# A first group of six columns, fewer GpSimd splits, two load queues, products of zeros and later latent norms in a two-layer decoder trunk

## The chip, the cores and the metric

The kernel runs on one core of one Trainium2 chip. The metric is the device time of one execution in microseconds (us), the median of several runs. The core has five engines with a row of instructions each: TensorE (PE: matrix products and transpositions; PEld is its weight load), VectorE (DVE), ScalarE (ACT), GpSimd (POOL) and SyncE (SP), which here issues loads and stores. An engine works through its own row in order; an instruction waits until what it needs from other engines is there, and all behind it wait too.

## The reference

A trunk of two layers over 512 tokens of width 1024, in fp32. Each layer normalises x, projects it by one wide matrix, feeds four causal token mixers, gates and sums their outputs, and ends with a SwiGLU block. Cut to what the change touches:

```python
for l in range(DEPTH):                      # DEPTH = 2
    h = rmsnorm(x, norm1_g[l])
    p = split_columns(h @ w_in[l])          # a_q ... c_q, c_kv, c_kr, d_q ... d_iq, d_ik, gate
    ...
    # C: q = rmsnorm(c_q) @ w_uq ; kv = rmsnorm(c_kv) @ w_ukv      (latents of 384 and 256 columns)
    # D: ik = apply_rope(rmsnorm(d_ik)) ; the index scores pick the keys
    # B: values b_vs, b_vw and gates b_g of the native sparse attention
    ...
    x = x + jnp.sum(g * br, axis=2) @ w_out[l]
    h2 = rmsnorm(x, norm2_g[l])
    gate, up = jnp.split(h2 @ w_gate_up[l], 2, axis=-1)
    x = x + (jax.nn.silu(gate) * up) @ w_down[l]
return rmsnorm(x, final_norm_g)
```

## The kernel before

x lies transposed, as eight tiles of 128 rows (model dimension) by 512 tokens. Every operand of a matrix product is split into a high and a low part (`fp32r`), and a product of two blocks is three instructions: high by high, high by low, low by high (`mm3`). "Product" below means one such instruction. A column of 128 outputs over eight tiles of x is so 24 products of 128x512.

**Weights.** They stream in as loads of 128x1024 (`raw`, three buffers), eight blocks each, in the order in which the code asks for blocks. `weights` (line 326) splits a half load, four blocks, at a time: ScalarE writes the high part `wp`, and VectorE subtracts for the low part; each third half is GpSimd's instead (`POOL_EVERY`). Six `wp` buffers take turns, and the splits run up to three halves ahead.

**The order.** Python code plays the program through once and writes the rows of all engines. A main path issues the products; beside it run tasks (generators) which `tick` advances when a planned time is due: a string that a task yields ("v", "a", "g", "p") means to come back when that engine's planned work is done, a number means so many us of planned time. These planned times set the order alone; on the chip only the order and the waits are left.

**PSUM.** Three banks `mm`, two `sc`, two `tr`, one `pv`. A bank given back in the code is reused by the next holder, which waits until the last reader is through.

**Start of a layer** (`mixers`, line 1264). `gather(GROUP)` makes the first GROUP columns one group: for each tile k of x the products of all these columns follow each other (`dense_group`, line 386). The first columns are the keys (c_kr with d_ik), three of c_q and two of c_kv. With a group of four, the two of c_kv follow one by one, 24 products each. Then come the token products (`native_values` by `values` and `dense_tokens`, line 414): x is the stationary side, 276 columns wide, one bank for each 128 tokens, in the order `mm`, `mm`, `pv`, `sc`; 12 products for each of eight tiles. Then the index queries `d_iq` (four columns) and gates.

**Norms.** h is fed unnormalised, and the scale is applied to the results. `rstd` (line 569) makes it: four small products with ones (a statistic, tile `tr<-ones,sq`), then on VectorE twelve small steps of 128x4 (`rx`, `ri`, `ry`, `ra`; here the "root"), then four transpositions `tr<-ident,ry`, from which ScalarE copies `R`. This is done for x, for the keys (`keys`, line 842), and for the latents c_q and c_kv (`latent`, line 1210, by `norm_row`, line 589). `plain` (line 833) multiplies a finished bank by R into `pl` and gives the bank back.

**Names in the rows.** `h` the split x, `sq` squares and their sums, `pl` a normalised column, `sh`, `rk`, `ro` the rope, `sk` and `kl` the high and low parts of the index keys, `lat` the normalised latents, `v`, `G`, `IW` the values and gates read from the token products' banks, `tab` rope tables, `z0` the zeros, `x0` the first x.

**Start of the program** (`run`, line 1512). GpSimd fills masks and constants (`setup`); SP issues, in this order, the first half load, `aux` (gains), the first tile of x, the second half load, and the other tiles of x with two loads between.

Of the kernel before, what the change touches and what calls it, by code (L numbers as in the profile page):

```python
# [11 lines left out]
F32 = mybir.dt.float32  # L12
F32R = mybir.dt.float32r
# [5 lines left out]
P = 128  # L19
S = 512  # L20
NQ = S // P
# [129 lines left out]

PL, LAT, BG, BGS = 1.0, 0.3, 5, 0.5
XR, TD, LD = 1.2, 6, 0.5
LOOK, ZC, NFT, GROUP = 3, 4, 16, 4
NKEEP = (NF - NFT) * KT // 4
N_U, N_RAW, N_WP, POOL_EVERY = 67, 3, 6, 3
BANKS = {"mm": 3, "sc": 2, "tr": 2, "pv": 1}


# [38 lines left out]
class Body:  # L198
# [127 lines left out]
    def weights(self, half):  # L326

        nc = self.nc
        total = 2 * NUNITS
        while self.nhalf <= min(half + min(LOOK, 1 + max(half, 0)), total - 1):  # L330
            h = self.nhalf
            while self.nraw <= min(h // 2 + N_RAW - 1, NUNITS - 1):
                self.load_raw()
            r = self.raws[h // 2][:, (h % 2) * S:(h % 2) * S + S]
            if h < total - NKEEP:
                w = self.sbt([P, 2, S], "wp", N_WP, "wp", F32R)
                w = w[:, 0, :], w[:, 1, :]
            else:
                w = self.pair("wk")
            self.wps[h] = w  # L340
            nc.scalar.activation(w[0], r, AF.Copy)
            pool = h % POOL_EVERY == POOL_EVERY - 1
            (nc.gpsimd if pool else nc.vector).tensor_tensor(w[1], r, w[0].bitcast(F32), op=ALU.subtract)
            if h % 2:
                del self.raws[h // 2]
            self.nhalf += 1
# [38 lines left out]

    def dense_group(self, group, pairs, k0=0, c=slice(0, S)):

        ps = [self.main_bank(tag) for tag in ("mm", "mm", "mm", "sc")[:len(group)]]
        last = len(pairs) - 1
        for k, x in enumerate(pairs):  # L390
            x = self.get(x)
            for i, (spec, cols, post, t) in enumerate(group):
                m = len(cols)
                w = self.block(spec[:2] + (k0 + k,), cols, spec[2:])
                self.mm3(ps[i][:m, c], w, (x[0][:, c], x[1][:, c]), k == 0, k == last)
                if k == last:
                    self.task(post(ps[i]), PL, t)
                self.tick()
# [167 lines left out]
            v.scalar_tensor_tensor(y, a, 1.5, y, op0=ALU.add, op1=ALU.mult)  # L566
        return y

    def rstd(self, sq, dim, rows=slice(0, P), blocks=range(NQ)):

        tr, ident = self.nc.tensor, self.ident
        ps = yield from self.bank("tr")
        yield from self.turn()
        for b in blocks:
            tr.matmul(ps[:, b:b + 1], sq[rows, b * P:(b + 1) * P], self.ones[rows, :], start=True, stop=True)
        yield 0.3
        n, b0 = len(blocks), blocks[0]
        col = self.rsqrt(ps[:, b0:b0 + n], n, dim)
        self.rel(ps)
        yield "v"  # L580
        yield 1.5
        ps = yield from self.bank("tr")
        yield from self.turn()
        for b in blocks:
            tr.transpose(ps[:, b * P:(b + 1) * P], col[:, b - b0:b - b0 + 1].to_broadcast([P, P]), ident)
        yield "p"
        return ps, col

    def norm_row(self, st, dim, n):
        yield from self.until(lambda: st.get("n") == n)  # L590
        yield "v"
        ps, col = yield from self.rstd(st["s"], dim)
        r = self.u("R")
        self.nc.scalar.activation(r, ps, AF.Copy)
        self.rel(ps)
        return r, col
# [32 lines left out]
        return out  # L629

    def load_tab(self, i):
        c, s = (self.sbt([P, S], "tab", 4, "tab") for _ in range(2))
        self.nc.sync.dma_start(c, self.tabs[i])
        self.nc.sync.dma_start(s, self.tabs[i + 1])
        return c, s
# [12 lines left out]
    def setup(self):  # L648
        nc, sb = self.nc, self.sb
        self.ident = sb.tile([P, P], F32, name="ident")  # L650
        nc.gpsimd.memset(self.ident, 1.0)
        nc.gpsimd.affine_select(out=self.ident, in_=self.ident, pattern=[[-1, P]], base=0, channel_multiplier=1,
                                compare_op=ALU.is_equal, fill=0.0)

        self.kls = [[sb.tile([P, S], F32R, name=f"kl{i}{h}") for h in range(2)] for i in range(2)]
        for kl in self.kls:
            for h in range(2):
                nc.gpsimd.memset(kl[h][64 - 64 * h:128 - 64 * h].bitcast(F32), 0.0)
        self.ones = sb.tile([P, 1], F32, name="ones")
        nc.vector.memset(self.ones, 1.0)  # L660

        self.TM = sb.tile([P, S], F32, name="TM")
        nc.gpsimd.memset(self.TM, 0.0)
        nc.gpsimd.affine_select(out=self.TM[:, S - P:], in_=self.TM[:, S - P:], pattern=[[-1, P]], base=0,
                                channel_multiplier=1, compare_op=ALU.is_ge, fill=BIG)

        self.CM = sb.tile([P, NQ, 32], F32, name="CM")
        nc.gpsimd.memset(self.CM, 0.0)
        for b in range(NQ):
            nc.gpsimd.affine_select(out=self.CM[:, b, :], in_=self.CM[:, b, :], pattern=[[-16, 32]],  # L670
                                    base=b * P - 31, channel_multiplier=1, compare_op=ALU.is_ge, fill=BIG)
        nc.gpsimd.memset(self.CM[:, :, 31:32], BIG)
        self.ZM = sb.tile([P, NQ], F32, name="ZM")
        nc.gpsimd.memset(self.ZM, 1.0)
        nc.gpsimd.affine_select(out=self.ZM, in_=self.ZM, pattern=[[P, NQ]], base=-31, channel_multiplier=1,
                                compare_op=ALU.is_ge, fill=0.0)

    def load_aux(self, l, eng=None):
        a = self.sb.tile([P, NAUX], F32, name=f"aux{l}", tag="aux", bufs=1)
# [162 lines left out]
    def keys(self, l, t1):  # L842

        nc = self.nc
        t1 = yield from self.aw(t1)
        tx = self.load_tab(TAB_X)
        hi, lo = slice(64, P), slice(0, 64)
        sq = self.u("sq")
        nc.scalar.activation(sq[hi], t1[hi], AF.Square)
        yield "a"  # L850
        ps, _ = yield from self.rstd(sq, 64, hi)
        rm = self.sbt([P, S], "xr", 3, "rm")
        nc.gpsimd.memset(rm[lo], 1.0)
        nc.scalar.activation(rm[hi], ps[hi], AF.Copy)
        self.rel(ps)
        yield "a"
        nc.vector.scalar_tensor_tensor(t1, t1, self.ax(l, "gm"), rm, op0=ALU.mult, op1=ALU.mult)
        r = yield from self.rope(t1, tx, self.u("rk"), False)
        ks = [self.stack_hi(r, h) for h in range(2)]
        yield "a"  # L860
        out = []
        for h, s in enumerate((lo, hi)):
            kl = self.u("kl", F32R)
            for o in (lo, hi):
                nc.gpsimd.tensor_tensor(kl[o], r[s], ks[h][s].bitcast(F32), op=ALU.subtract)
            out.append((ks[h], kl))
        yield "g"
        return out
# [341 lines left out]
    def latent(self, l, ts, dim, gname):  # L1210

        st, xs = {}, []
        for t in ts:
            x = yield from self.aw(t)
            xs.append(x)
            sq = self.norm_sq(x)
            yield "a"
            self.norm_add(st, sq)
        r, _ = yield from self.norm_row(st, dim, len(ts))
        yield "a"  # L1220
        out = []
        for i, x in enumerate(xs):
            self.nc.gpsimd.tensor_tensor(x, x, r, op=ALU.mult)
            yield "g"
            out.append(self.task(self.split(x, self.ax(l, gname, i), "lat"), 0))
        return out
# [185 lines left out]
    def out_proj(self, l, src, ap):  # L1412
        nc = self.nc
        st = {}
        xs, hs = [], []
        self.gather(3)
        for m in range(KT):
# [5 lines left out]
                yield "v"  # L1423
                return (yield from self.feed(l, "g2", m, x, st))
            xr = self.xr
            xr[m] = self.sbt([P, S], "xr", 3, "xr")
            nc.sync.dma_start(xr[m], src[m])
            hs.append(self.queue(("out", l), np.arange(m * P, (m + 1) * P), ap, post))
        return xs, hs, st
# [82 lines left out]
    def run(self):  # L1512
        nc = self.nc
        st = {}
        self.xr = {}
        self.setup()
        xs = [self.u("x0") for _ in range(KT)]
        r = self.raws[0] = self.sbt([P, 1024], "raw", N_RAW, "raw")
        nc.sync.dma_start(r[:, :S], self.wstream[0][:, :S])
        self.load_aux(0)  # L1520
        nc.sync.dma_start(xs[0], self.xT[0])
        nc.sync.dma_start(r[:, S:], self.wstream[0][:, S:])
        self.nraw = 1
        for m in range(1, KT):
            nc.sync.dma_start(xs[m], self.xT[m])
            if m in (2, 4):
                self.load_raw()
        self.weights(-1)
        self.H = [self.task(self.feed(0, "g1", m, x, st), XR * m) for m, x in enumerate(xs)]
        self.tick()  # L1530
# [2 lines left out]
        for l in range(DEPTH):  # L1533
# [5 lines left out]
            st = {}  # L1539
# [62 lines left out]
```

## Time and profile before

| | us |
|---|---|
| median of 3 runs (2273.11 to 2275.95) | 2274.15 |
| the profiled execution's own time | 2274.43 |
| its span, first to last instruction | 2272.6 |
| TensorE busy in it | 2222.0 (98%) |
| VectorE busy | 1400.4 (62%) |
| ScalarE busy | 928.9 (41%) |
| GpSimd busy | 656.0 (29%) |

The profile is one execution. Times in it count from the span's start. A row of a timeline gives the start, how long a run of equal instructions lasted together, the engine, the line, the operation, the written and the read tiles by name, the shapes and the count; in brackets how long the engine had been idle before it and what ended that. Matrix products are pipelined, so the last of a run overlaps the next run by some 0.1 to 0.2 us: distances between starts are the better measure. All instructions bear line 185, that of the helper which records them.

### The profile page before, as it was taken

The page shows a single profiled execution, that of the slowest core. Times are in us where ns is not written, and L with a number is a line of the kernel's source. Part 1 is how long each engine was busy: PE and PEld are TensorE (multiplying, and loading weights), DVE is VectorE, ACT ScalarE, POOL GpSimd, SP SyncE. Part 2 cuts the span into 40 slices and gives each one's busy share as a digit, 9 for nine tenths or more (in the row PEclk, how much of TensorE's full clock was granted, in tenths as well). Part 3 has the DMA queues.
Part 4 walks back from the last instruction along what each step waited for, and adds up shares of the span by engine and source line. Part 5 has one row for each costly group of instructions (what it writes and reads, how often), then busy time and mean ns, then how long its engine had stood idle before and what let it go on. Part 6 is the DMA issues. An engine that isn't in the chain of part 4 may idle for free.

```text
span 2272.6 us, 29756 instructions
## 1 busy us (share of the span) xinstructions
PE 2222.0 (98%) x11080; PEld 1850.7 (81%) x11080; DVE 1400.4 (62%) x2837; ACT 928.9 (41%) x1907; POOL 656.0 (29%) x494
## 2 busy tenths in 40 slices
PE   8899999999999999999989999999999999999997
PEld 6789788778888788888878897887888888888887
DVE  6877898976655533233468778988865464332234
ACT  4456454434443432223334654544444433222233
POOL 3622333421431222122144222233124312222122
PEclk9999999999999999999999999999999999999999
DMA  4332233211223323233333222422222233333322
GB/s 158 94 92 66 75 118 100 80 56 57 77 81 104 122 94 96 90 93 96 122 107 102 75 66 84 124 88 72 61 65 76 84 125 95 95 93 93 102 84 75
DMA packets 61792, 206.55 MB, mean 91 GB/s; under 512 B 6736, under 2 KB 9040, under 8 KB 61648
## 3 DMA queue, kind: packets, MB, share of 16 engines
q1 hardware_dynamic: 61648, 204.66, 29.3%
q8 instruction: 87, 1.43, 0.3%
q14 instruction: 57, 0.47, 0.1%
HBM read 200.44 MB, written 4.19 MB: 90 GB/s over the span
## 4 chain that ended last, share of the span: by engine, by line
PE 85%; DVE 11%; issue 2%; ACT 1%; POOL 1%; DMA 0%; SPq 0%; DVEq 0%; POOLq 0%; ACTq 0%
PE mm L185 74%; PE sc L185 5%; PE pv L185 4%; PE tr L185 3%; DVE wp L185 2%; DVE dm L185 1%; DVE e L185 1%; DVE sq L185 1%; DVE ra L185 1%; DVE sm L185 1%; DVE sc L185 1%; DVE m L185 0%; DVE sh L185 0%; DVE ry L185 0%; ACT wp L185 0%
## 5 line engine op out<-in xcount | busy, mean ns | idle before, releaser
L185 PE MATMUL mm<-h,wp 128*128 128x512 f32 x5232 | 1283.5, 398 | 6.9 <-ACT h L185 6.1
L185 PEld LDWEIGHTS mm<-h,wp 128*128 128x128 f32 x5232 | 969.8, 189 | 223.4 <-ACT h L185 6.1
L185 POOL TENSOR_TENSOR wp<-raw,wp 128x512 fp32r<-128x512 f32 x236 | 327.3, 1387 | 1088.9 <-ACT wp L185 1038.0
L185 DVE TENSOR_TENSOR wp<-raw,wp 128x512 fp32r<-128x512 f32 x474 | 397.9, 842 | 189.2 <-ACT wp L185 188.4
L185 ACT ACTIVATE wp<-raw 128x512 fp32r<-128x512 f32 x710 | 422.4, 622 | 166.0 <-PE mm L185 150.2
L185 PE MATMUL mm<-hid,wp 128*128 128x512 f32 x912 | 213.3, 395 | 0.0
L185 PEld LDWEIGHTS mm<-hid,wp 128*128 128x128 f32 x912 | 171.2, 188 | 41.6
L185 ACT ACTIVATE e<-sc,mn 128x128 f32<-128x128 f32 (+1 forms) x192 | 99.3, 524 | 140.5 <-DVE mn L185 132.9
L185 POOL TENSOR_TENSOR sh<-sh,tab 128x512 f32<-128x512 f32 x60 | 80.8, 1347 | 174.2 <-DVE sh L185 174.1
L185 PE MATMUL mm<-wp,h 128*128 128x256 f32 (+1 forms) x864 | 119.2, 290 | 0.5 <-DVE ro L185 0.5
L185 POOL TENSOR_TENSOR z<-z,R 128x512 f32<-128x512 f32 x44 | 57.9, 1316 | 212.2 <-ACT z L185 212.1
L185 PEld LDWEIGHTS mm<-wp,h 128*128 128x128 f32 x864 | 110.6, 193 | 1.2 <-DVE ro L185 0.7
L185 DVE TENSOR_TENSOR z<-mm,R 128x512 f32<-128x512 f32 x44 | 30.4, 692 | 131.5 <-PE mm L185 131.5
L185 DVE TENSOR_TENSOR z<-mm,z 128x512 f32<-128x512 f32 x44 | 30.4, 691 | 128.6 <-PE mm L185 128.6
L185 ACT ACTIVATE pt<-tr 128x384 fp32r<-128x384 f32 (+1 forms) x120 | 62.3, 526 | 105.5 <-PE tr L185 96.6
L185 DVE TENSOR_TENSOR x<-mm,x 128x512 f32<-128x512 f32 (+1 forms) x40 | 23.3, 584 | 126.0 <-PE mm L185 126.0
L185 PEld LDWEIGHTS pv<-pt,v 128*128 128x128 f32 x720 | 93.3, 189 | 8.5 <-issue 2.6
L185 ACT ACTIVATE hid<-z 128x512 fp32r<-128x512 f32 x44 | 27.9, 634 | 166.7 <-DVE z L185 166.7
L185 ACT ACTIVATE z<-z 128x512 f32<-128x512 f32 x44 | 28.0, 636 | 163.0 <-DVE z L185 163.0
L185 PE MATMUL pv<-pt,v 128*128 128x256 f32 x720 | 93.3, 276 | 0.4 <-DVE pt L185 0.4
L185 PE MATMUL mm<-ap,wp 128*128 128x512 f32 x384 | 89.8, 395 | 0.0
L185 DVE CUSTOM_DVE_ANT_0 sc<-sc,TM 128x128 f32<-128x128 f32 (+3 forms) x168 | 78.2, 500 | 17.0 <-PE sc L185 16.2
(206 smaller groups left out, 2680.2 us busy)
## 6 DMA issues: line engine op xcount, KB each, us to landing
raw<-wstream SPq DMA_DIRECT2D x360, 512.0 KB, 3.6
tab<-tabs SPq DMA_DIRECT2D x16, 256.0 KB, 4.2
x<-xT SPq DMA_DIRECT2D x8, 256.0 KB, 6.6
xr<-xT SPq DMA_DIRECT2D x8, 256.0 KB, 3.9
spill<-x SPq DMA_DIRECT2D x8, 256.0 KB, 2.2
xr<-spill SPq DMA_DIRECT2D x8, 256.0 KB, 4.2
outT<-o SPq DMA_DIRECT2D x8, 256.0 KB, 2.3
raw<-wstream SPq DMA_DIRECT2D x2, 256.0 KB, 4.1
```

Of the source, the lines that this page charges most:

```text
L185: return f(*args, **kw)
```

## The change

- `GROUP` goes from 4 to 6: the first group of a layer takes the keys, c_q and c_kv together, its last two columns in a second `sc` bank and in `pv`.
- GpSimd splits no halves before half 12 (of the whole program), that is during layer 0's first group; VectorE does these.
- `aux` is loaded by ScalarE's queue, and `setup` is called behind the loads in the code.
- `warm` fills a tile with zeros on VectorE and issues nine products of it into bank `pv` ahead of all others.
- For the latents the task waits 3.0 planned us ahead of the statistic and 8.0 instead of 1.5 between root and transpositions.
- `tab`, `rm` and `xr` tiles come from the common pool `u`, which grows from 67 to 74 tiles.

```diff
-LOOK, ZC, NFT, GROUP = 3, 4, 16, 4
+LOOK, ZC, NFT, GROUP = 3, 4, 16, 6
+NWARM = 9
-N_U, N_RAW, N_WP, POOL_EVERY = 67, 3, 6, 3
+N_U, N_RAW, N_WP, POOL_EVERY = 74, 3, 6, 3
...
-            pool = h % POOL_EVERY == POOL_EVERY - 1
+            pool = h % POOL_EVERY == POOL_EVERY - 1 and h >= 2 * GROUP
...
-        ps = [self.main_bank(tag) for tag in ("mm", "mm", "mm", "sc")[:len(group)]]
+        ps = [self.main_bank(tag) for tag in ("mm", "mm", "mm", "sc", "sc", "pv")[:len(group)]]
...
-    def rstd(self, sq, dim, rows=slice(0, P), blocks=range(NQ)):
+    def rstd(self, sq, dim, rows=slice(0, P), blocks=range(NQ), slack=1.5):
...
-        yield 1.5
+        yield slack
...
-    def norm_row(self, st, dim, n):
+    def norm_row(self, st, dim, n, ahead=0.0, slack=1.5):
         yield from self.until(lambda: st.get("n") == n)
         yield "v"
-        ps, col = yield from self.rstd(st["s"], dim)
+        yield ahead
+        ps, col = yield from self.rstd(st["s"], dim, slack=slack)
...
-        c, s = (self.sbt([P, S], "tab", 4, "tab") for _ in range(2))
+        c, s = self.u("tab"), self.u("tab")
...
+    def warm(self):
+
+        z = self.u("z0", F32R)
+        self.nc.vector.memset(z.bitcast(F32), 0.0)
+        ps = self.take("pv")
+        for i in range(NWARM):
+            self.tc.nc.tensor.matmul(ps, z[:, :P], z, start=i == 0, stop=i == NWARM - 1)
+        self.rel(ps)
...
-        rm = self.sbt([P, S], "xr", 3, "rm")
+        rm = self.u("rm")
...
-        r, _ = yield from self.norm_row(st, dim, len(ts))
+        r, _ = yield from self.norm_row(st, dim, len(ts), 3.0, 8.0)
...
-            xr[m] = self.sbt([P, S], "xr", 3, "xr")
+            xr[m] = self.u("xr")
...
-        self.setup()
         xs = [self.u("x0") for _ in range(KT)]
         r = self.raws[0] = self.sbt([P, 1024], "raw", N_RAW, "raw")
+        self.load_aux(0, self.tc.nc.scalar)
         nc.sync.dma_start(r[:, :S], self.wstream[0][:, :S])
-        self.load_aux(0)
         nc.sync.dma_start(xs[0], self.xT[0])
         nc.sync.dma_start(r[:, S:], self.wstream[0][:, S:])
+        self.warm()
...
+        self.setup()
         self.weights(-1)
```

The rows of the engines move as follows. The rows of before carry line 185, those of after line 186.

VectorE in layer 0's first group, from the second half's split (`wp_26`, now `wp_30`) on, before:

```order
L185 TENSOR_TENSOR wp_26_153<-raw_9_110,wp_26_153 128x512
L185 TENSOR_TENSOR sq_22_145<-sq_19_139,sq_22_145 128x512
L185 SCALAR_TENSOR_TENSOR h_24_148<-x0_3_104,aux0_112,h_23_147 128x512
L185 TENSOR_TENSOR sq_25_151<-sq_22_145,sq_25_151 128x512
L185 SCALAR_TENSOR_TENSOR h_28_165<-x0_4_105,aux0_112,h_27_164 128x512
L185 TENSOR_TENSOR wp_34_185<-raw_10_118,wp_34_185 128x512
L185 TENSOR_TENSOR sq_29_171<-sq_25_151,sq_29_171 128x512
L185 SCALAR_TENSOR_TENSOR h_31_178<-x0_5_106,aux0_112,h_30_177 128x512
```

and VectorE at the same place now:

```order
L186 TENSOR_TENSOR wp_30_167<-raw_9_74,wp_30_167 128x512
L186 TENSOR_TENSOR sq_26_159<-sq_23_153,sq_26_159 128x512
L186 SCALAR_TENSOR_TENSOR h_28_162<-x0_3_68,aux0_75,h_27_161 128x512
L186 TENSOR_TENSOR sq_29_165<-sq_26_159,sq_29_165 128x512
L186 SCALAR_TENSOR_TENSOR h_32_179<-x0_4_69,aux0_75,h_31_178 128x512
L186 TENSOR_TENSOR wp_37_196<-raw_12_94,wp_37_196 128x512
L186 TENSOR_TENSOR wp_38_199<-raw_12_94,wp_38_199 128x512
L186 TENSOR_TENSOR sq_33_185<-sq_29_165,sq_33_185 128x512
L186 SCALAR_TENSOR_TENSOR h_35_192<-x0_5_70,aux0_75,h_34_191 128x512
```

Both halves of a load are split here now; up to the last sum `sq_53` VectorE has 19 rows, seven of them splits.

TensorE at the start of layer 0's token products (`x<-wp,h` 128x276), before; `tr_104` is the transposition of c_q's root:

```order
L185 MATMUL tr_104_512<-ident_66,ry_96_473 128x128 x4
L185 MATMUL mm_107_519<-wp_86_422,h_13_130 128x276 x2
L185 MATMUL mm_107_519<-wp_86_422,h_14_131 128x276
L185 MATMUL mm_108_520<-wp_86_422,h_13_130 128x276 x2
L185 MATMUL mm_108_520<-wp_86_422,h_14_131 128x276
L185 MATMUL pv_109_521<-wp_86_422,h_13_130 128x276 x2
```

and TensorE at the same place now, from the group's last product (column six, bank `pv`) on; `tr_89` is the keys' statistic:

```order
L186 MATMUL pv_22_152<-h_50_243,wp_71_377 128x512
L186 MATMUL tr_89_461<-ones_114,sq_81_446 128x1 x4
L186 MATMUL mm_87_459<-wp_73_394,h_15_142 128x276 x2
L186 MATMUL mm_87_459<-wp_73_394,h_16_143 128x276
L186 MATMUL mm_88_460<-wp_73_394,h_15_142 128x276 x2
L186 MATMUL mm_88_460<-wp_73_394,h_16_143 128x276
L186 MATMUL pv_99_490<-wp_73_394,h_15_142 128x276 x2
```

The keys' statistic moved from within c_kv's first column to between the group and the token products, and `pv` is used by the group and soon again.

VectorE at this place, where `pl` reads the banks of columns five and six, now; the rows ahead are the end of the keys' root:

```order
L186 TENSOR_TENSOR ra_95_480<-ry_92_470 128x4
L186 SCALAR_TENSOR_TENSOR ra_95_480<-ra_95_480,rx_90_466 128x4
L186 SCALAR_TENSOR_TENSOR ry_92_470<-ra_95_480,ry_92_470 128x4
L186 TENSOR_TENSOR pl_96_484<-sc_21_151,R_70_364 128x512
L186 TENSOR_TENSOR pl_98_488<-pv_22_152,R_70_364 128x512
L186 TENSOR_TENSOR wp_101_492<-raw_68_356,wp_101_492 128x512
```

and behind the keys' root before:

```order
L185 TENSOR_TENSOR wp_86_422<-raw_60_305,wp_86_422 128x512
L185 TENSOR_TENSOR sq_84_418<-sq_76_387,sq_84_418 128x512
L185 TENSOR_TENSOR sq_87_432<-sq_84_418,sq_87_432 128x512
L185 TENSOR_TENSOR wp_89_442<-raw_60_305,wp_89_442 128x512
L185 TENSOR_TENSOR pl_92_454<-mm_69_367,R_64_336 128x512
```

The two `pl` of c_kv stand right behind the keys' root.

TensorE at the transposition of c_kv's root (`tr_140`) before, among the token products:

```order
L185 MATMUL pv_109_521<-wp_118_566,h_36_198 128x276 x2
L185 MATMUL pv_109_521<-wp_118_566,h_37_199 128x276
L185 MATMUL tr_140_674<-ident_66,ry_126_609 128x128 x4
L185 MATMUL sc_110_522<-wp_118_566,h_36_198 128x276 x2
L185 MATMUL sc_110_522<-wp_118_566,h_37_199 128x276
```

and the transpositions of both latents' roots (`tr_150`, `tr_153`) now, in the second column of `d_iq`:

```order
L186 MATMUL mm_137_698<-h_50_243,wp_132_660 128x512
L186 MATMUL mm_148_761<-h_15_142,wp_134_677 128x512
L186 MATMUL mm_148_761<-h_16_143,wp_134_677 128x512
L186 MATMUL mm_148_761<-h_15_142,wp_134_677 128x512
L186 MATMUL tr_150_768<-ident_103,ry_121_613 128x128 x4
L186 MATMUL mm_148_761<-h_24_155,wp_134_677 128x512
L186 MATMUL mm_148_761<-h_25_156,wp_134_677 128x512
L186 MATMUL mm_148_761<-h_24_155,wp_134_677 128x512
L186 MATMUL tr_153_781<-ident_103,ry_128_643 128x128 x4
```

They moved behind all token products and 27 and 30 products of `d_iq`; `mm_148` takes the bank of `mm_87`.

VectorE at the end of the second latent root now:

```order
L186 TENSOR_TENSOR ra_131_653<-ry_128_643 128x4
L186 SCALAR_TENSOR_TENSOR ra_131_653<-ra_131_653,rx_126_639 128x4
L186 SCALAR_TENSOR_TENSOR ry_128_643<-ra_131_653,ry_128_643 128x4
L186 TENSOR_TENSOR wp_132_660<-raw_104_512,wp_132_660 128x512
L186 TENSOR_TENSOR wp_134_677<-raw_110_556,wp_134_677 128x512
L186 TENSOR_TENSOR wp_146_730<-raw_117_601,wp_146_730 128x512
L186 SCALAR_TENSOR_TENSOR v_140_709<-mm_87_459,ry_62_316,v_139_708 128x256
L186 TENSOR_SCALAR G_85_457<-mm_87_459,ry_62_316 128x12
```

Both roots of the latents stand in one piece ahead of these rows in layer 0; before, c_q's root stood much earlier.

## Rows read from the trace of the kernel before

**Rows 1.** The first line of the profile's page.

```profile
span 2272.6 us, 29756 instructions
```

**Rows 2.** What TensorE waited for in the whole span: the waiting instruction, whose result it waited for, us in total, times, the longest.

```profile
PE tr L185 <- DVE ry L185: 13.1, 3, 6.0
PE tr L185 <- DVE sq L185: 8.3, 6, 3.5
```

**Rows 3.** Stretches of ten us: length, busy us and count of PE, PEld, DVE, ACT and POOL, then the granted TensorE clock as a share of full, DMA share and GB/s.

```profile
0.00:10.00 10.00, 3.92 (x10) 2.82 (x11) 2.32 (x5) 5.04 (x8) 5.07 (x20) 1.00 0.78 264
...
20.00:30.00 10.00, 6.48 (x26) 4.98 (x25) 8.19 (x21) 1.08 (x2) 1.28 (x1) 0.83 0.35 105
...
70.00:80.00 10.00, 10.00 (x48) 9.08 (x48) 5.92 (x15) 4.39 (x9) 4.65 (x3) 0.79 0.54 157
...
1190.00:1200.00 10.00, 7.25 (x37) 7.04 (x38) 6.53 (x10) 3.95 (x9) 5.47 (x4) 0.66 0.33 105
```

**Rows 4.** Timeline of TensorE in layer 0's first group.

```profile
6.08 4.00 PE L185 MATMUL mm<-h,wp 128*128 128x512 f32 x9 [6.08 <-ACT h L185]
...
11.07 2.62 PE L185 MATMUL mm<-h,wp 128*128 128x512 f32 x9 [0.29 <-ACT wp L185]
...
25.11 1.05 PE L185 MATMUL tr<-ones,sq 128*128 128x1 f32 x8 [3.52 <-DVE sq L185]
...
28.44 2.85 PE L185 MATMUL mm<-h,wp 128*128 128x512 f32 x9
```

**Rows 5.** Timeline of the other engines there: SP's issue of `aux`, ScalarE's second h and second split, VectorE's sums, h and a split, a GpSimd split, the last two sums.

```profile
1.25 0.42 SPq L680 DMA_DIRECT2D aux<-aux  x1
...
8.12 0.72 ACT L185 ACTIVATE h<-x,aux 128x512 fp32r<-128x512 f32 x1 [1.57 <-DMA x<-xT]
...
10.40 0.61 ACT L185 ACTIVATE wp<-raw 128x512 fp32r<-128x512 f32 x1
...
15.84 0.68 DVE L185 TENSOR_TENSOR sq<-sq,sq 128x512 f32<-128x512 f32 x1
...
16.44 0.74 DVE L185 SCALAR_TENSOR_TENSOR h<-x,aux,h 128x512 fp32r<-128x512 f32 x1
...
17.10 0.68 DVE L185 TENSOR_TENSOR sq<-sq,sq 128x512 f32<-128x512 f32 x1
17.20 1.74 POOL L185 TENSOR_TENSOR wp<-raw,wp 128x512 fp32r<-128x512 f32 x1 [2.43 <-ACT wp L185]
...
17.70 1.78 DVE L185 TENSOR_TENSOR wp<-raw,wp 128x512 fp32r<-128x512 f32 x1
...
23.65 1.41 DVE L185 TENSOR_TENSOR sq<-sq,sq 128x512 f32<-128x512 f32 x2
```

**Rows 6.** Timeline in layer 0 at the keys' statistic and its root, and the last transposition ahead of the token products.

```profile
40.07 1.05 PE L185 MATMUL tr<-ones,sq 64*128 64x1 f32 x8
...
41.05 4.46 PE L185 MATMUL mm<-h,wp 128*128 128x512 f32 x18
41.16 0.16 DVE L185 TENSOR_SCALAR rx<-tr 128x4 f32<-128x4 f32 x1 [2.39 <-PE tr L185]
...
43.42 0.69 DVE L185 TENSOR_TENSOR wp<-raw,wp 128x512 fp32r<-128x512 f32 x1
...
51.56 0.60 PE L185 MATMUL tr<-ident,ry 128*128 128x128 f32 x4
...
51.91 1.01 PE L185 MATMUL mm<-wp,h 128*128 128x276 f32 x6
```

**Rows 7.** Timeline in layer 0's token products, at c_kv's root and its transposition, and the products behind them.

```profile
59.99 0.92 PE L185 MATMUL mm<-wp,h 128*128 128x276 f32 x6
60.07 5.80 POOL L185 TENSOR_TENSOR kl<-rk,sk 64x512 fp32r<-64x512 f32 x4
60.58 0.15 DVE L185 TENSOR_SCALAR rx<-tr 128x4 f32<-128x4 f32 x1
...
60.76 0.54 PE L185 MATMUL pv<-wp,h 128*128 128x276 f32 x3
...
68.80 1.08 PE L185 MATMUL tr<-ident,ry 128*128 128x128 f32 x4 [5.98 <-DVE ry L185]
...
71.75 0.89 PE L185 MATMUL pv<-wp,h 128*128 128x276 f32 x3
...
72.44 0.89 PE L185 MATMUL sc<-wp,h 128*128 128x276 f32 x3
...
75.12 23.86 PE L185 MATMUL mm<-h,wp 128*128 128x512 f32 x102
```

**Rows 8.** Timeline in layer 1: the first products, the keys' statistic, VectorE's first row behind the keys' root, the two waits, and the first products behind the token products.

```profile
1136.29 2.26 PE L185 MATMUL mm<-h,wp 128*128 128x512 f32 x9
...
1162.79 1.05 PE L185 MATMUL tr<-ones,sq 64*128 64x1 f32 x8
...
1167.10 0.68 DVE L185 TENSOR_TENSOR sq<-sq,sq 128x512 f32<-128x512 f32 x1
...
1181.66 1.02 PE L185 MATMUL tr<-ones,sq 128*128 128x1 f32 x8 [1.83 <-DVE sq L185]
...
1192.75 1.09 PE L185 MATMUL tr<-ident,ry 128*128 128x128 f32 x4 [4.61 <-DVE ry L185]
...
1198.63 23.88 PE L185 MATMUL mm<-h,wp 128*128 128x512 f32 x102
```

## The prediction

> **What bounds the kernel now.** The profiled execution took 2274.43 us, of which the span is 2272.6 [rows 1]; that is 0.3 above the median of the runs, 2274.15. The sum below is made against 2274.4. I read TensorE's waits first: it is busy nearly throughout, so only the few places where it stands still can be bought back. Two lines of the list [rows 2] hold 21 us: transpositions waiting for the last step of a reciprocal root (`ry`) and statistics waiting for a sum of squares (`sq`). Then the table of stretches [rows 3]: the granted clock is below 1 in 20:30, 70:80 and 1190:1200, each time behind such a wait. Then the timeline of these places [rows 4 to 8].
>
> Outside them nothing is won: the two orders of TensorE's instructions differ only in about the first 250 rows, in the same stretch of layer 1, and by the place of two products. So I price three places, each by what it took less what its work takes without waits. One 128x512 product takes 0.234 us (102 in 23.86), a 276-wide one 0.128 (six from 59.99 to 60.76) [rows 7]; a column of statistics takes 0.98 (40.07 to 41.05), its transposition 0.35 (51.56 to 51.91) [rows 6].
> - A, layer 0 from 11.07 to 51.91 = 40.8 us: 132 products (30.9) and three statistics with transposition (4.0). Lost: 5.9, of which 3.52 is the wait at 25.11 and most of the rest low clock behind it (nine products in 2.85 at 28.44, where nine at 0.234 are 2.1) [rows 4, 6].
> - B, the token products from 51.91 to 75.12 = 23.2: 96 x 0.128 = 12.3, and 1.3. Lost: 9.6, of which 5.98 is the wait at 68.80; behind it three products take 0.69, not 0.38 (71.75 to 72.44) [rows 7].
> - C, layer 1 from 1136.29 to 1198.63 = 62.3: 144 products 33.7, tokens 12.3, four statistics 5.3. Lost: 11.0, of which 1.83 and 4.61 are waits [rows 8].
>
> **Part A after.** Moving the load of `aux` to ScalarE's queue takes one issue of 0.42 us out of SP's row ahead of every load of x [rows 5]; ScalarE's issue lies in its idle start. ScalarE stood 1.57 us for the second x at 8.12, and the split of the second half at 10.40 follows that without a gap [rows 5], so I take 0.4 us earlier, 10.0. The DMA share is 0.78 there already [rows 3], so it may be nothing: 0 to 0.4. The Trainium skill (DMA: Bandwidth & Descriptors, "Issuing engines are not separate DMA queues") says that queues of different engines run on the same 16 DMA engines, so that a second queue saves only issue time; by it the 0.4 is the most, and with 0 the sum below would be 0.4 less.
>
> Nine products took 4.00 us at the start of before, which is the low clock although the column reads 1.00 [rows 3, 4]; if the nine of zeros begin at 1.4 (an estimate: behind the fill of their tile), they end at 5.4, ahead of the first real product. They buy no time: products of the first half then end earlier, but column five needs the second half, whose split is at 10.0. A new wait of up to 2 us takes the place of slow products there (bounds -0.5 to +1.5, I take +0.5 for a low clock behind that wait).
>
> From 10.6 on TensorE has the same 132 products. Ahead of the statistic now stand 51 of them (11.9 us) instead of 42. VectorE has 19 wide operations from the second split to the last sum, 13 at 0.60 and 6 at 0.66 (15.84, 16.44, 17.10 [rows 5]): 11.8 us, no longer with the three stalls of about 1.1 which a GpSimd split caused (17.70 took 1.78 beside 17.20). The sum is there at 22.4, TensorE at 23.4: the wait of 3.52 and the low clock go. The added splits cost one wait: the sixth of the 19 is the split that product 13 needs, at 14.3, and TensorE is there at 13.4: 0.9. **A loses 1.4 instead of 5.9 and starts 0.4 earlier: 4.9 won** (3 to 6).
>
> **Part B after: a wait takes the place of another.** The sixth column of the group now sits in the one bank `pv`, and the token products need `pv` as third. VectorE frees it with `pl`, and in the new order both last `pl` stand behind the twelve small steps of the keys' root, which wait for the statistic TensorE issues right behind the group. Before, from the start of such a statistic (40.07) VectorE was through its steps at 43.42 [rows 6]; two `pl` more (0.60 and 0.69) make 4.64 us. TensorE has only the statistic and six products until then, 1.75. **New wait: 2.9 us**, certain but for its size. Low clock behind it: B before lost 2.8 beyond its two waits of 0.78 and 5.98 (0.78 is in the second line of [rows 2]), so 0 to 2.8; I take 1.4, since one shorter wait stands behind it.
>
> The latent transpositions move behind the first 27 products of the next columns, so the wait of 5.98 goes. But VectorE still does both roots in a row, and now behind them come the split `wp_132` and the `v`, `G`, `IW` operations that free bank `mm` for the second of those columns. A root takes 2.3 us alone (41.16 to 43.42) and 8.2 beside GpSimd's `kl` (60.58 to 68.80) [rows 6, 7]. In layer 0 GpSimd has the two rope steps and a split beside the first root, then waits for ScalarE: I take 4 and 2.5 us. From the start of the keys' statistic the first root begins at 14.4, `wp_132` is split at 22, and TensorE, itself late by 4.3, wants it at 23; the bank is free at 26, wanted at 25.4. I take 0.9 for both (0 to 4). **B loses 5.2 instead of 9.6: 4.4 won** (1.5 to 6.7).
>
> **Part C after.** The same, with a GpSimd split beside the keys' root: there VectorE was through only at 1167.10, 4.31 us behind 1162.79 [rows 8]; with two `pl` 5.6, less 1.75: **3.85 us wait**, and 1.8 for the clock. The order puts a split and all four `kl` straight behind the rope on GpSimd, so the first root takes near 8 us (from 16 to 24 behind the statistic): 0.8 of wait for the split behind it. The second root, two splits and the first `v` follow (2.3 + 1.2 + 0.8): the bank comes at 28.2, TensorE wants it at 26.2: 2.0 more. With 0.3 of small ones C loses 8.7 instead of 11.0: **2.3 won** (-1.5 to 7).
>
> **Other edits.** `tab`, `rm` and `xr` now draw from the pool `u`, which has seven tiles more: the same space. Some of these loads wait in SP's row for TensorE, with weight loads queued behind them, but for products that lie well ahead of the neighbouring loads' own waits: nothing. The `lat` operands come some 15 us later; their first reader is eight columns of 24 products (45 us) on: nothing. The zeros' bank is `pv`, first used by the group's column six: free by then.
>
> Sum: 4.9 + 4.4 + 2.3 = 11.6; 2274.4 - 11.6 = **2263 us**.
>
> **Rivals.**
> 1. The latent wait goes and no bank or split comes late: then only 2.9 and 3.85 remain with little low clock, and A 5.5 + B 6.5 + C 7 = 19 are won: 2255. For it: in B VectorE and TensorE come out within 1 us of each other. Against: waits of 1.83 already brought the clock down.
> 2. The waits only change place: the `pv` wait, the low clock and the late bank cost in B and C as much as the old waits; A alone stays: 2269. For it: the second price in C rests on one order of GpSimd and may be as high in B.
> 3. Slower: both roots run at the pace of 8.2 us [rows 7] in both layers, because GpSimd has rope, split, `kl` and split in a row. Then `wp_132` comes 16 us behind 14.4 and the bank at 34, wanted at 25: B loses 9 + 5 and the clock again, 16 in all (-6), C likewise 18 (-7), and A gives 5: -8, 2282. It is slower from where the two roots together take over 13 us. Against: in layer 0 GpSimd must wait for ScalarE's four `sk` before `kl`.
> 4. A does not do what it says: the sum of squares is late still, the drops stay: 2268.
>
> **How the numbers follow.** The forecast gets 0.60, rival 1 0.17, rival 2 0.14, rival 3 0.04, rival 4 0.05. The bounds of the parts give 2274.4 - 19.7 = 2255 to 2274.4 - 3 = 2271; with rival 1 inside and rival 3 out I say 2254 to 2271. A measurement of this kernel tells 0.2%, 4.5 us, from no change, so faster means below 2269.6: the forecast, rival 1, half of rivals 2 and 4: 0.86; same 0.10; slower 0.04.
>
> **What would show it.** A: the first statistic without a wait and clock 1 in 20:30; if it waits over 1 us, my count of VectorE's steps is wrong. B: a wait of TensorE's `pv` token products for `pl`, near 2.9 us in layer 0 and 3.9 in layer 1, with a low clock behind; if it is absent the `pl` are not where I put them. The transpositions of `ry` for the latents without a wait. A wait of a `mm` product for `v` or `IW`, near 2 us, in layer 1; near 10 us in both layers would be rival 3. If the part behind 80 us in layer 0 takes longer than before, I overlooked who waits for the later `lat`.

## The result, and the profile after

The changed kernel takes 2251.64 us (median of 4 runs, 2250.64 to 2252.9), the kernel before 2275.05 (4 runs, 2273.11 to 2277.41): a ratio of 0.9899, 95% interval 0.9886 to 0.9911. That is 23.4 us, twice the 11.6 forecast, and below the range. The profiled execution took 2250.64 us, 23.8 less than that of before [rows 1].

The first line of the changed kernel's page:

```profile
span 2248.4 us, 29760 instructions
```

What TensorE waited for in it, as in [rows 2]:

```profile
PE sc L186 <- ACT re L186: 7.1, 5, 3.9
PE pv L186 <- DVE pl L186: 6.3, 2, 3.7
PE tr L186 <- DVE e L186: 5.6, 4, 2.2
PE mm L186 <- DVE wp L186: 4.3, 2, 2.8
PE mm L186 <- DVE IW L186: 3.2, 2, 1.7
...
PE tr L186 <- DVE ry L186: 2.5, 1, 2.5
...
PE tr L186 <- DVE sq L186: 1.5, 1, 1.5
```

`ry` and `sq` fell from 21.4 to 4.0 us, but `re`, `pl`, `wp` and `IW` together, nearly absent before, now hold 20.9. TensorE stands idle for 49.4 us of its span (2248.4 less 2199.0 busy), before for 50.6. So the waits cannot be the 23.8 us. The stretches, with the columns of [rows 3], first of the changed kernel:

```profile
20.00:30.00 10.00, 10.00 (x51) 8.39 (x50) 7.08 (x21) 2.27 (x4) 1.82 (x2) 1.00 0.34 107
40.00:50.00 10.00, 7.33 (x40) 6.49 (x39) 7.95 (x21) 4.41 (x8) 1.84 (x2) 0.86 0.18 48
...
90.00:100.00 10.00, 5.25 (x20) 3.74 (x19) 9.91 (x10) 5.65 (x11) 8.63 (x6) 0.92 0.34 105
900.00:1000.00 100.00, 100.00 (x438) 82.10 (x437) 32.44 (x46) 26.24 (x45) 23.02 (x17) 1.00 0.32 95
```

and the last of these of the kernel before:

```profile
900.00:1000.00 100.00, 100.00 (x430) 80.45 (x429) 29.80 (x42) 25.98 (x44) 21.60 (x16) 1.00 0.30 95
```

From 900 to 1000 TensorE stands in the SwiGLU block of layer 0, in both kernels busy all the time, at full granted clock, with the same two kinds of product; yet it takes 438 of them where it took 430. From start to start a product takes 228.9 ns there, as the mean of the stretch, and took 233.3: 1.9% less, far from any row that the change moves. That is what the prediction did not see.

The start of layer 0 on TensorE, which answers to [rows 4, 6, 7]:

```profile
1.53 4.21 PE L686 MATMUL pv<-z 128*128 128x512 f32 x9 [1.53 <-DVE ones L186]
5.94 0.60 PE L186 MATMUL mm<-h,wp 128*128 128x512 f32 x1 [0.20 <-ACT h L186]
...
21.84 0.94 PE L186 MATMUL tr<-ones,sq 128*128 128x1 f32 x8
...
41.84 1.05 PE L186 MATMUL tr<-ones,sq 64*128 64x1 f32 x8
42.81 1.02 PE L186 MATMUL mm<-wp,h 128*128 128x276 f32 x6
46.51 0.65 PE L186 MATMUL pv<-wp,h 128*128 128x276 f32 x3 [2.67 <-DVE pl L186]
...
61.81 3.38 PE L186 MATMUL mm<-h,wp 128*128 128x512 f32 x14
66.65 2.58 PE L186 MATMUL mm<-h,wp 128*128 128x512 f32 x10 [1.46 <-DVE wp L186]
70.81 0.94 PE L186 MATMUL mm<-h,wp 128*128 128x512 f32 x3 [1.57 <-DVE IW L186]
```

The first statistic waits for nothing; the wait for `pl` stands where the prediction put it; the split and the bank are late behind it. Then comes a place that the prediction did not price, the index products (`sc<-sk,sq`). All engines there:

```profile
91.23 1.74 POOL L186 TENSOR_TENSOR wp<-raw,wp 128x512 fp32r<-128x512 f32 x1
...
92.93 1.73 POOL L186 TENSOR_TENSOR sh<-sh,tab 128x512 f32<-128x512 f32 x1
...
94.74 1.59 POOL L186 TENSOR_TENSOR ro<-ro,sh 128x512 f32<-128x512 f32 x1
...
96.36 1.28 ACT L186 ACTIVATE sq<-ro 64x512 fp32r<-64x512 f32 x2 [3.69 <-POOL ro L186]
97.67 0.66 ACT L186 ACTIVATE re<-sc 128x256 f32<-128x256 f32 x2
98.10 0.50 PE L186 MATMUL sc<-sk,sq 128*128 128x384 f32 x1 [3.87 <-ACT re L186]
```

TensorE needs a bank that ScalarE's `re` frees; `re` stands behind `sq<-ro`, which waits for GpSimd's last rope step `ro`. What put GpSimd back, in its own timeline:

```profile
76.56 3.08 POOL L186 TENSOR_TENSOR pl<-pl,R 128x512 f32<-128x512 f32 x2
...
83.02 3.46 POOL L186 TENSOR_TENSOR pl<-pl,R 128x512 f32<-128x512 f32 x2
...
89.53 1.74 POOL L186 TENSOR_TENSOR pl<-pl,R 128x512 f32<-128x512 f32 x1
```

These five are the latents' normalisation. Before, they ran among the token products (in layer 0 from 55.4 to 74.0); the later norms put them among the rope of `d_iq`.

### The profile page after: what moved, and what is told of

Its sections match the earlier page's. It is cut to its first block, busy times and chain, and to the rows that moved or that the text cites. A ratio compares the mean times of both kernels' runs of the same rounds, so it can differ in the third digit from the quotient of the medians.

```text
span 2248.4 us, 29760 instructions
## 1 busy us (share of the span) xinstructions
PE 2199.0 (98%) x11089; PEld 1849.3 (82%) x11089; DVE 1402.6 (62%) x2842; ACT 929.9 (41%) x1907; POOL 655.5 (29%) x490
## 4 chain that ended last, share of the span: by engine, by line
PE 84%; DVE 11%; issue 2%; ACT 1%; POOL 1%; DMA 0%; SPq 0%; DVEq 0%; POOLq 0%
PE mm L186 72%; PE sc L186 5%; PE pv L186 4%; PE tr L186 3%; DVE wp L186 2%; DVE e L186 1%; DVE sq L186 1%; DVE ra L186 1%; DVE sh L186 1%; DVE sm L186 1%; DVE dm L186 1%; DVE lat L186 1%; DVE sc L186 1%; DVE ry L186 0%; DVE m L186 0%
## 5 line engine op out<-in xcount | busy, mean ns | idle before, releaser
L186 PE MATMUL mm<-h,wp 128*128 128x512 f32 x5136 | 1246.4, 396 | 9.6 <-DVE wp L186 4.3
L186 PEld LDWEIGHTS mm<-h,wp 128*128 128x128 f32 x5136 | 953.2, 189 | 208.5 <-DVE wp L186 5.7
```

Of the source, the lines that this page charges most:

```text
L186: return f(*args, **kw)
```

## The experiments

**Where the 24 us come from.** Two theories stood against the forecast's: that the pace of TensorE hangs on where its operands lie in SBUF, and that it hangs on the rows ahead of it. Tiles get their places in the order in which the code first asks for them. `setup`'s tiles (512 + 4 x 2048 + 32 + 2048 + 512 + 32 = 11328 bytes a partition, which is 44 x 256 + 64) lay below the pool `u` before; the later call puts them above it. In bytes behind a multiple of 256, `u` lies at 224 before and at 160 after, `wp` at 96 in both. `u` holds the moving side of most products (h), `wp` the stationary one: they lie 128 apart before and 64 after. I call this their distance.

Run e1, on the kernel before:

```diff
-        self.setup()
         xs = [self.u("x0") for _ in range(KT)]
...
+        self.setup()
         self.weights(-1)
```

> The kernel before with one line moved: `setup()` is called behind the loads in the code, as in the changed kernel. Every engine's row of instructions stays as it was; what changes is where tiles lie in SBUF, since the pool `u` is now taken first and starts 11328 bytes lower. Theory of the place (TensorE's pace hangs on where its operands lie): the stretch 900:1000 holds 438 matrix instructions and not 430, and some 7,400 products of 512 columns gain 3.3 to 4.4 ns each, 24 to 33 us: 2242 to 2251 us. Theory of the order (the gain of the change comes from the moved rows, as I predicted): nothing moves but names, 2275 us and 430. Theory of the stream (the pace hangs on the 18 rows more that TensorE has ahead of all products): 2275 us and 430 too.

Measured: 2253.48 us, ratio 0.9908 (0.9894 to 0.9923). This one line, which moves no row of any engine, gives nearly all that the change gives; it ends a little above its theory's 2242 to 2251 us.

Run e2, the changed kernel with that line undone:

> The changed kernel with `setup()` called first again, so that the pool `u` starts where it did before and the buffers `wp` stay where the change has them; the other edits stay. Theory of the place: 430 matrix instructions in 900:1000 again, and the 24 to 33 us come back: 2276 to 2285 us, no faster than the kernel before. Theories of the order and of the stream: 438 and 2252 us.

Measured: 2275.32 us, ratio 1.0002 (0.9992 to 1.0012). The rest of the change, all that the prediction priced, is worth nothing that these runs can tell. The stretch of e1, then of e2:

```profile
900.00:1000.00 100.00, 100.00 (x438) 82.07 (x437) 31.04 (x44) 26.98 (x46) 21.28 (x16) 1.00 0.32 95
```

```profile
900.00:1000.00 100.00, 100.00 (x431) 80.42 (x430) 31.06 (x44) 26.44 (x45) 21.30 (x16) 1.00 0.31 92
```

Run e3 (the changed kernel without the call of `warm`) and run e4 (an unused tile of 96 bytes ahead of `u`, so that all the operands move together):

> The changed kernel without the products of zeros (their tile is left out too; no result changes). Theory of the stream: TensorE's 18 rows are gone, so 430 matrix instructions in 900:1000, and 2276 to 2285 us. Theory of the place: 438 as in the changed kernel. Then only the start counts: without the zeros the first products run at the low clock (nine took 4.00 us before), but the group waits for x and splits anyway: 0 to 3 us more, 2252 to 2255 us.

> The changed kernel with an unused tile of 96 bytes a partition ahead of the pool `u`: all tiles of `u`, `raw`, `aux` and `wp` move up by 96 bytes together, and `u` starts at a multiple of 256. Rows are the same. Theory of the place, if the address itself counts: the number in 900:1000 leaves 438, by as much as 8 either way as far as the two kernels show, so 2225 to 2285 us. If only the distance between the operands counts, or no place at all: 438 and 2252 us.

Measured: 2252.38 us (0.9889 to 0.9919) and 2252.36 (0.9886 to 0.9916), with 438 and 439 products in the stretch: it is neither the rows ahead nor the place of `u` as such. The products of zeros are worth less than these runs can tell.

Run s1 measures the pace by itself:

> A kernel of products alone, which leaves the whole reference out: 48 products of 128x512 for each of 96 pairs of places, in the kernel's pattern (high by high, high by low, low by high; four blocks of weights in turn), nothing beside them on any engine or queue. In the first 64 pairs the moving side starts at 0, 32, 64, ... 2016 behind a multiple of 2048 bytes, with the stationary side 864 behind one, as `wp` lies in all kernels so far; in the last 32 the moving side lies at 160 and then at 1248, as in the changed kernel and in the one before, and the stationary side at 0, 32, ... 480. Theory of the address: the spacing of the products follows the moving side's place, 0.2289 us at 160 and 0.2333 at 1248. Theory of the distance: 0.2333 comes back wherever the two sides lie as far apart as in the kernel before (384 modulo some power of two), so the last 32 pairs show it too. Theory of the traffic (the pace hangs on where the other engines and the loads write at the same time): all 96 alike, at 0.2289 or below.

Measured, as the mean spacing of the last 43 products of each pair, the 96 pairs sorted by distance (moving start less stationary start, modulo 256 bytes), 12 pairs each:

```
distance     0      32      64      96      128          160     192     224
ns         226.7   233.3   228.9   233.4   232.4-233.3  234.3   233.3   233.3
```

Each column's pairs agree within 0.2 ns, whichever side was moved, but for 128: 233.3 where the moving side was shifted, 232.4 where the stationary one was. So it is the distance, and a case that no kernel had yet, 0, is the fastest. Three pairs as stretches, at distances 0, 64 and 128; the length of each, its second column, is what 48 products took:

```profile
51.54:62.45 10.91, 10.91 (x50) 9.01 (x48) 0.00 (x0) 0.00 (x0) 1.00 0.01 2
73.65:84.65 11.00, 11.00 (x50) 9.01 (x48) 0.00 (x0) 0.00 (x0) 1.00 0.01 1
95.86:107.06 11.20, 11.20 (x50) 9.01 (x48) 0.00 (x0) 0.00 (x0) 1.00 0.00 0
```

Runs e7 (the changed kernel, 64 bytes between `u` and `wp`: distance 0), e8 (the kernel before, 128 bytes: distance 0) and e9 (the kernel before, 64 bytes: distance 64) put this to use with one line each, here that of e7:

```diff
+        self.sb.tile([P, 16], F32, name="gap")
         self.weights(-1)
```

> The changed kernel with an unused tile of 64 bytes a partition between the pool `u` and `wp`: both now lie 160 bytes behind a multiple of 256, so the distance of moving and stationary side is 0 there, where it was 64. Theory of the distance: products of 512 columns at 0.2267 us and not 0.2289, 441 in 900:1000; some 7,400 of them give 16 us: 2235 us. Rival (in the full kernel other things than the distance bound the pace at 0.2289): 438 and 2251 us.

> The kernel before, all its rows as they were, with an unused tile of 128 bytes a partition between the pool `u` and `wp`: distance 0 instead of 128. Theory of the distance: 0.2267 us instead of 0.2324 to 0.2333, 441 instead of 430 in 900:1000, some 7,400 products give 42 to 49 us: 2225 to 2233 us, far below the changed kernel. Rival (the pace hangs on the moving side's place, which stays here): 2274 us and 430.

> The kernel before with 64 bytes between `u` and `wp`: distance 64, as in the changed kernel, by another way than the changed kernel's. Theory of the distance: 438 in 900:1000, some 7,400 products give 25 to 33 us: 2241 to 2249 us, and no slower than the changed kernel. Rival (it is the lower start of `u`, not the distance): 2274 us and 430.

Measured: e7 2243.84 us, ratio 0.9864 (0.9849 to 0.9878); e8 2245.37, 0.9868 (0.9851 to 0.9884); e9 2255.18, 0.9913 (0.9899 to 0.9928). The direction is the theory's, the pace too (443 and 442 in the stretch, of e7 and of e8; 226.7 ns from start to start in both, what s1 gave at distance 0, as the kernel before and the changed one have what it gave at 128 and 64):

```profile
900.00:1000.00 100.00, 100.00 (x443) 82.79 (x442) 32.03 (x45) 27.27 (x47) 24.07 (x18) 1.00 0.32 96
```

```profile
900.00:1000.00 100.00, 100.00 (x442) 82.78 (x442) 31.75 (x45) 27.50 (x47) 23.63 (x18) 1.00 0.31 95
```

The sizes are not: 19 to 24 us (e9, e1, e2) and not 25 to 33 for 128 to 64, 8 to 11 (e7, e8, and e10 below) and not 16 for 64 to 0. I had priced all 7,400 products, and these alone. A part is shown by the products of 128x256 in which the two sides change places, x stationary and `wp` moving: busy time of all 768 in the span, of the kernel before, the changed one and e7:

```profile
L185 PE MATMUL mm<-wp,h 128*128 128x256 f32 x768 | 101.3, 285 | 0.5 <-DVE ro L185 0.5
...
L186 PE MATMUL mm<-wp,h 128*128 128x256 f32 x768 | 98.6, 282 | 0.5 <-DVE ro L186 0.5
...
L186 PE MATMUL mm<-wp,h 128*128 128x256 f32 x768 | 102.0, 286 | 0.6 <-DVE ro L186 0.6
```

They are fastest in the changed kernel and slowest where the distance is 0: 3.4 of the 16 us go there (e8 has 101.9, e9 98.9). The order that s1 found holds for products of 512 columns with `wp` as the stationary side, not for these.

Another part is lost to other engines. In e9's trace the 2000th product, at 401 us before, comes 1.4 us earlier, and the 2500th, at 503, 0.2. That is in layer 0's mixers, where VectorE is busy for 78 to 87% of each 100 us from 100 to 500: there TensorE is idle for 9.5 us and not 7.9, and in 490:500 its granted clock is 0.83 and not 1.00. The first product of layer 1 comes 10.5 us earlier (1125.79, before 1136.29 [rows 8]), so nearly all of that was won behind 500 us. What is left of the difference no run takes apart.

**Where the gain of the rows went.** With equal distance, e2 against before, four landmarks of TensorE tell it (starts of the first product of each kind, from the timelines; then the length of the index stretch, from the first index product to the first of the latents):

| | index, layer 0 | latents | stretch | layer 1 | index | latents | stretch |
|---|---|---|---|---|---|---|---|
| before | 98.81 | 126.23 | 27.4 | 1136.29 | 1222.35 | 1248.66 | 26.3 |
| e2 | 91.47 | 124.84 | 33.4 | 1131.81 | 1218.27 | 1250.52 | 32.3 |
| changed | 89.66 | 123.29 | 33.6 | 1119.98 | 1204.53 | 1235.92 | 31.4 |
| e5 | 90.30 | 123.26 | 33.0 | 1118.28 | 1202.83 | 1235.98 | 33.2 |
| e6 | 92.81 | 121.19 | 28.4 | 1117.89 | 1207.00 | 1234.53 | 27.5 |
| e11 | 89.72 | 119.22 | 29.5 | 1114.34 | 1199.73 | 1231.01 | 31.3 |
| e12 | 90.42 | 122.61 | 32.2 | 1117.75 | 1203.13 | 1233.47 | 30.3 |

In e2 7.3 us are won by the first index product, and 6.0 given back in each layer's index stretch. Five runs ask why. Run e5 puts the latents' normalisation behind the rope:

```diff
         r, _ = yield from self.norm_row(st, dim, len(ts), 3.0, 8.0)
         yield "a"
+        yield 20.0
```

> The changed kernel with 20 planned us between the latents' roots and their normalisation: the five `pl` that GpSimd multiplies by R and the five `lat` of VectorE stand behind the rope of `d_iq` now, instead of among it. TensorE's row changes in the places of a few products only. Theory of the queue on GpSimd (the index products wait for `re`, that for `sq` of the rope, that for GpSimd's `ro`, which stands behind five `pl` of 1.7 us): the waits for `re` of 7.1 us and the low clock behind them go, 4 to 6 us in each layer of which the late operands may give back 2: 2240 to 2247 us. Rival (the rope comes late because TensorE's columns do, and the `pl` fill gaps): 2250 to 2253 us, and a wait for `re` of 3 to 4 us stays near 95.

Measured: 2251.79 us (0.9881 to 0.9910), in the rival's range. The theory of GpSimd's queue falls in this form: the stretch stays as long, since `re` now stands behind ScalarE's `lat` and behind a `th` that waits 3.65 us for VectorE (TensorE waits 2.66 at 112.56). The work costs as much there.

Run e6 takes the later norms back (`len(ts)` without `3.0, 8.0`), the places unchanged:

> The changed kernel with the latents' statistics and transpositions at their old planned distances (0 and 1.5 us); all else, the places in SBUF too, as in the changed kernel. My prediction's step (this edit takes away the wait of TensorE for the latents' roots): the transpositions stand among the token products again and wait 4 to 6 us for `ry` in each layer, less the 3 us of each layer for late banks and splits: 2253 to 2260 us. Rival (the edit gains nothing, since the `pl` pushed among the rope cost as much): 2250 to 2253 us, with the wait for `re` smaller than 3.9 us.

Measured: 2250.39 us (0.9876 to 0.9909), no slower than the changed kernel and in the rival's range. Its waits:

```profile
PE tr L186 <- DVE ry L186: 9.4, 2, 6.9
...
PE sc L186 <- ACT re L186: 2.7, 4, 1.2
```

The later norms take 6.9 us of waits for `ry` away and put 4.4 of `re` in place of them, with the low clock behind. By the landmarks they win 3.2 and 4.6 us ahead of the index products and lose 5.2 and 3.9 behind: at this distance the wait only changes place.

Runs e11 and e12, the changed kernel without the ten `pl` of GpSimd, and with them on VectorE:

> The changed kernel without GpSimd's multiplication of the latents by R: the ten `pl` (five a layer, 1.66 us each) are left out, so the latents stay unnormalised; all else and the places stay. Theory of the queue on GpSimd (these `pl` stand among the rope of `d_iq`, and the index products wait for what comes behind them): the waits for `re` of 3.9 us near 95 and their like in layer 1, with the low clock behind them, go: 5 to 6 us a layer, 2240 to 2242 us. Rival (it is VectorE's and ScalarE's work on `lat`, or the columns coming late): 2250 to 2252 us, with the waits for `re` where they were.

> The changed kernel with these ten `pl` on VectorE instead of GpSimd; nothing is left out. Theory of the queue on GpSimd: as without them, less what 3.5 us more on VectorE cost: 2242 to 2246 us. Rival (any engine of the rope that takes the latents' work there is late): 2248 to 2254 us, a wait for `re` or for `IW` and `v` of 3 us or more stays in each layer.

Measured: e11 2248.11 us, 0.9880 (0.9865 to 0.9894); e12 2250.16, 0.9887 (0.9872 to 0.9902). Without these rows layer 0's stretch is 4.1 us shorter, layer 1's is not, and the waits for `re` fall from 7.1 to 5.9 only:

```profile
PE sc L186 <- ACT re L186: 5.9, 4, 1.9
```

So e11 misses its 2240 to 2242 us, and these `pl` are two thirds of the longer stretch in layer 0 (4.1 of 6.2 us). That it is GpSimd's queue, and not their work wherever it is done, is not shown: on VectorE they leave a stretch of 32.2, near the 33.6 of the changed kernel, and 2250.16 us lies in the rival's range. What holds layer 1's stretch up is not settled: the same chain over `ro`, `sq` and `re` is late there, with VectorE's `lat` among the rope as well; no run took that out alone.

Runs e10 (e6 with 64 bytes between `u` and `wp`) and e13 (e10 with the `pl` on VectorE) look for the best version:

> The changed kernel with the latents' norms at their old distances and the 64 bytes between `u` and `wp`. Theory of the distance with rows that add up: 16 us below the same rows at distance 64, 2250.4 - 16 = 2234 us, within 2 of the changed rows at distance 0. If a faster TensorE now waits more for the same splits and roots: up to 5 us of the 16 lost, 2239 us.

> The changed kernel with the norms of the latents at their old distances, their `pl` on VectorE, and 64 bytes between `u` and `wp`. Theory of the queue on GpSimd: 2 to 4 us below the same kernel with `pl` on GpSimd (2239.6), 2235 to 2238 us. Rival (VectorE's five `pl` come ahead of `v`, `G` and `IW`, which free the banks of `d_iq`'s columns): 2240 to 2245 us, with waits for these banks of over 3 us a layer.

Measured: e10 2239.59 us, 0.9845 (0.9830 to 0.9859), the lowest of all, below both kernels, and where it was expected if TensorE waits more. At distance 0 the order does count: e10 lies 4.3 us below e7 (2238.37 to 2240.63 against 2243.53 to 2244.23), which differs by the later norms alone, and 5.8 below e8 (2243.68 to 2246.79), which has the rows of before. There the other edits of the rows do gain, and the later norms give most of it back; at distance 64 e6 shows 1.3 us of this, less than these runs can tell.

e13 takes 2245.22, 0.9868 (0.9852 to 0.9885), close to what its rival said, with VectorE's `pl` ahead of the bank's readers, 3.9 us in one layer and 2.0 in the other:

```profile
PE mm L186 <- DVE IW L186: 5.9, 2, 3.9
```

## Why the prediction was wrong

Its direction was right for a reason that it did not have. Two steps failed, both in "Other edits", where I took nothing.

- **"the same space"**. The step failed in counting bytes and not places, and the later call of `setup`, which moves no row, was not priced at all. It is the 64 bytes by which `u` moved against `wp` that are worth 23.7 us (e2 to the changed kernel). The sentence ahead of the parts, that outside three places nothing is won because TensorE's rows are the same there, failed with it: the same rows took 0.2289 us each and not 0.2333.
- **The `lat` operands "come some 15 us later; ... nothing"**. I asked who reads them, not what they stand ahead of on GpSimd, VectorE and ScalarE. The index stretches of e2 are 6.0 us longer in both layers: 12 lost. The runs show that the later norms cause most of it (e6: 28.4 and 27.5, where the changed kernel has 33.6 and 31.4). The prediction's last sign of being wrong, a longer part behind 80 us in layer 0, pointed at these operands, and the index stretch is that part.

The three places, by e2, whose products last as long as before's:

- **A** won 5.8, forecast 4.9 (3 to 6). From the 13th product (10.51 and three of 0.234, 11.2) to 44.44 are 33.2 us, and its work without waits is 33.2: both the wait for `sq` and the low clock went, and the 0.9 for the split did not come. TensorE started 0.1 later, not 0.4 earlier.
- **B**: the wait for `pl` was 2.68 us, forecast 2.9, and the low clock behind it 1.7, forecast 1.4 (44.44 to 63.42 is 19.0, its work 14.6). But the late split and bank, one term of 0.9 (0 to 4), cost 3.4: 63.42 to 74.59 holds 30 products and two transpositions, 7.7 us of work. B won 1.8, not 4.4.

```profile
44.44 1.02 PE L186 MATMUL mm<-wp,h 128*128 128x276 f32 x6
48.14 0.95 PE L186 MATMUL pv<-wp,h 128*128 128x276 f32 x3 [2.68 <-DVE pl L186]
...
63.42 3.43 PE L186 MATMUL mm<-h,wp 128*128 128x512 f32 x14
68.19 2.60 PE L186 MATMUL mm<-h,wp 128*128 128x512 f32 x10 [1.35 <-DVE wp L186]
72.33 0.93 PE L186 MATMUL mm<-h,wp 128*128 128x512 f32 x3 [1.55 <-DVE IW L186]
...
74.59 17.04 PE L186 MATMUL mm<-h,wp 128*128 128x512 f32 x72
```

- **C**: the wait for `pl` was 3.63, forecast 3.85; the split behind the roots cost 2.74 and not 0.8, and the bank's 2.0 did not come. From 1131.81 to 1202.09, 30 products of `d_iq` in, are 70.3 us; before needed 62.3 and 7.0 [rows 8]. C lost 0.9 where a gain of 2.3 was forecast, inside its bounds.

The three make 6.7 us, not 11.6, inside the bounds of the parts. With the 12 lost at the index products the rows come out slower by 5, and 3 that e2's trace gains between 125 and 1132, where the rows are the same, leave 2; one execution each does not tell more, and by the runs it is none (a ratio of 1.0002). Rival 2, that the waits only change place, is what the rows did, but at a place that it did not name, so that A's gain went too.

## What to carry to other kernels

Before pricing a change by its rows, compare the pace of products that it does not touch, in a stretch where TensorE never waits; if that differs, look at where operands lie, since a moved allocation is an edit of its own. Lay the moving and stationary operands of the most frequent dense products so that their starts agree modulo 256 bytes, and measure it: here, for products of 512 columns, an unused tile of 64 or 128 bytes was worth more than all the reordering (e8: 29 us), while products of 256 columns with the sides exchanged lost a little. And of a step that is moved, ask at its new place which engine's row it stands ahead of, and who waits at that row's end.

## What the runs showed of the hardware

The spacing of products of 128x512 in fp32r, a weight load beside each, hangs on the distance of the two operands' starts modulo 256 bytes: 226.7 ns at 0, 228.9 at 64, 232.4 to 234.3 at the other steps of 32 that were tried, with every other engine idle and the clock granted in full. The Trainium skill (SBUF — State Buffer, "Who interferes with whom") gives TensorE two read ports, one for the moving operand and one for weight loads, and calls them independent; here the pace depends on where the two operands lie to each other, and the measurement decides. What in the memory makes it so no run shows. For products of 128x256 with the sides exchanged the kernels' own traces show another order: 768 of them take 98.6 us in the changed kernel, 101.3 in the one before and 102.0 in e7, where the distance is 0. Other types, and steps below 32 bytes, were not tried.
